# Who rounds and who subtracts the experts' weights: one engine fewer in the weight split of a mixture of experts

## The chip, the cores and the metric

One core of one Trainium2 chip. The metric is the device time of one execution in microseconds (us). Three runs of the kernel before give a median of 2515.39 us (2513.58 to 2515.87). All durations in this text are microseconds unless marked ns.

The engines are named as in the profile: PE is TensorE (PEld its weight loads), DVE is VectorE, ACT is ScalarE, POOL is GpSimd, SP is SyncE, which only issues DMAs here.

## What is computed

The reference runs two blocks over one sequence of 1024 tokens of width 1024. The first block is two layers of gating and sparse attention. The second is a windowed attention with a short convolution, and then a mixture of experts, which is where the change lies:

```
hierarchical_moe(h, ...):                      # 1024 tokens, 32 experts, top 2 of one group each
    expert, gates = router(h)                  # 2048 assignments of a token to an expert
    for e in range(32):
        xb  = h[tokens of expert e]            # gathered rows
        hid = silu(xb @ w_gate[e]) * (xb @ w_up[e])    # w_gate, w_up: 1024 x 256
        out[tokens of e] += gates * (hid @ w_down[e])  # w_down: 256 x 1024
```

Everything is in float32, and the weights are read once: 32 experts of three matrices of 1 MB.

## The kernel before, in words

**Products in parts.** A float32 product is made of three matmuls on rounded parts. Each operand is split into `hi`, its value rounded to the matmul's format, and `lo`, what is left of it. `mm3` (lines 99 to 102) then sums hi by hi, hi by lo and lo by hi; in the profile these are lines L100, L101 and L102. The split itself is the helper `split` (line 104): a rounding copy by POOL (L106), ACT (L108) or DVE, and then a subtraction, source minus hi, on L111 by DVE or POOL. All splits of the kernel share these lines, so the experts' splits are told apart by their tile, `ew`.

**The experts' stage** is the last fifth of the kernel. It runs from about 2050 to the end at 2515. For each expert:
- `load_e` (line 1506, its DMA on L1514) loads the three weight matrices, 1 MB each, through SP's queue into a ring of 11 places (`NRAW`). A load waits until its place is free, that is until both halves of the matrix loaded 11 loads earlier have been split, and until the third load before it has landed (`AHEAD = 3`).
- `gather` (L1604) fetches the expert's tokens, up to 96 rows, with an indirect DMA that POOL issues, three experts ahead.
- `prep` (line 1618) turns the tokens round with eight transposes (L1624), rounds them on ACT (L1626) and subtracts on DVE (L1627), into `xT`.
- `split_e` (line 1609) splits a weight matrix into a tile `ew`, of which there are three. It does so in two halves of 128 partitions by 1024 values. So there are six roundings and six subtractions per expert.
- `gate_up` (line 1630) makes the gate and up products, 48 matmuls of 256 columns into bank `sm`; ACT takes the tanh (L1638) and DVE finishes `th` (L1639, L1640).
- `hidden` (line 1645) transposes `th` (L1648), rounds (ACT, L1650) and subtracts (DVE, L1651) into `hdT`.
- `down` (line 1654) makes the down product, 12 matmuls of 512 columns into bank `big`; ACT scales the result into `yt` (L1663), and POOL issues the indirect DMA that adds its rows to the output (L1664, the scatter).

**Who splits what.** A counter `sc` goes round six places, one step per half:

```
HI_E = ("act", "act", "act", "pool", "act", "act")
        i = sc[0] % 6
        split(w_[:, 0, c], w_[:, 1, c], raw[:, c], HI_E[i], G if i in (1, 5) else V)
```

From the second expert on, the order of the calls puts each half of an expert in a fixed place. The second halves of gate and up are subtracted by POOL, and the second half of down is rounded by POOL; the other five roundings are ACT's and the other four subtractions DVE's.

**Order.** Each engine runs its instructions in a fixed order, one after the other. The program's order is expert by expert (`for e in range(NE)`, the loop behind `finish`): products of expert e, tokens and gate and up weights of e + 1, down product of e - 1, hidden part and down weights of e. The build (`schedule_with_timeline_sim=True`, line 1764) may shift instructions among each other by a simulated timeline of the engines, from which each engine's final order comes. After the loop stands a second one (`For_i`, over the blocks of experts with more than 96 tokens); with these inputs it is not entered: the profile shows 128 subtractions of DVE on `ew`, four for each of 32 experts.

Of the kernel before, what the change touches and what calls it, by code (L numbers as in the profile page):

```python
# [28 lines left out]
BIG = 1e30  # L29
SL = 96          # tokens of one expert's block  # L30
# [10 lines left out]
def tile_hybrid(ctx, tc, I, out):  # L41
# [7 lines left out]
    banks = {}  # L49
    psum2 = ctx.enter_context(tc.tile_pool(name="psum2", bufs=2, space=PSUM))  # L50

    def bank_plan(big, half, sm, tr, sc=0):
        """Banks of PSUM: big tiles of two, the others of one. Two small and two transposed ones stay in place."""
        if banks:
            banks["stack"].close()
        st = ExitStack()
        banks.update(stack=st, pool=st.enter_context(tc.tile_pool(name="psum", bufs=2, space=PSUM)),
                     big=big, half=half, sm=sm, tr=tr, sc=sc, turn={"sm": 0, "tr": 0})
# [54 lines left out]
    # weights are streamed two 128-row blocks at a time and split one step ahead of their use  # L113
# [11 lines left out]
    # the number of stages whose loads wait for an instruction, and which  # L125
# [33 lines left out]
    # background work, placed between the steps of a product. Generators in bgs yield about the time they take.  # L159
    # Streams hold the vector engine's long chains: they yield the time they take there and whether what comes next  # L160
    # starts on the tensor engine, which then must not come up before the chain is done. now is the tensor engine's
    # time so far, dve that up to which the vector engine has work.
# [97 lines left out]
    def dense_T1(KT, rhs, evac, bgt=1300.0):  # L260
        """One block of 128 channels: the halves take turns so that two banks last."""
        ps = [None, None]
        for k0 in range(0, KT, 4):
            hi, lo = wnext()
            hi, lo = (x.rearrange("p a b -> p (a b)").rearrange("p (k c) -> p k c", c=128) for x in (hi, lo))
            for h in range(2):
                c = slice(h * 512, (h + 1) * 512)
                if k0 == 0:
                    ps[h] = bank([128, 512], "half")
                for kk in range(4):  # L270
                    k = k0 + kk
                    mm3(ps[h], hi[:, kk], lo[:, kk], rhs(k, 0)[:, c], rhs(k, 1)[:, c], start=(k == 0),
                        stop=(k == KT - 1))
                if k0 + 4 == KT:
                    evac(h, ps[h])
                bg(bgt, 12 * 512 / 2.4)
# [14 lines left out]
    # every streamed weight, in the order of use  # L291
# [20 lines left out]
    # ------------------------------------------------------------------ block 1  # L312
# [9 lines left out]
    # rotary tables  # L322
# [29 lines left out]
    # modulation rows  # L352
# [13 lines left out]
    # first layer: scale and shift as columns, and h straight into its transposed halves. The products for 256 channels  # L366
    # of one of them are summed over row blocks by the vector engine, by the two slow ones or by the tensor engine.
# [77 lines left out]
    # later modulation rows: products summed over row blocks by the vector engine, over rows by one product with ones  # L445
# [63 lines left out]
    def rope(dst, src, t, H, eng):  # L509
        """Rotary embedding of H heads of 64 channels; t is one tile, or None for all tiles with one head each."""  # L510
        if t is None:
            cw, sw = cosT, sinT
        else:
            cw = cosT[:, t:t + 1, :].to_broadcast([128, H, 32])
            sw = sinT[:, t:t + 1, :].to_broadcast([128, H, 32])
        a, b = slice(0, 32), slice(32, 64)
        tb = tmp.tile([128, H, 64], FT, name="s2")
        eng.tensor_tensor(tb[:, :, a], src[:, :, b], sw, op=OP.mult)
        eng.tensor_tensor(tb[:, :, b], src[:, :, a], sw, op=OP.mult)
        for c in (a, b):  # L520
            eng.tensor_tensor(dst[:, :, c], src[:, :, c], cw, op=OP.mult)
        eng.tensor_tensor(dst[:, :, a], dst[:, :, a], tb[:, :, a], op=OP.subtract)
        eng.tensor_tensor(dst[:, :, b], dst[:, :, b], tb[:, :, b], op=OP.add)
# [35 lines left out]
    def layer(l, xin, hT=None):  # L559
# [6 lines left out]
        # keys, values, index keys and index weights  # L566
# [22 lines left out]
        # index queries  # L589
# [20 lines left out]
        def select(i):  # L610
            """Bias of query tile i: 0 at its 256 largest index scores, first ones on ties, else -BIG."""
# [30 lines left out]
            # upper halves of the scores as integers: they rise with the scores where these are non-negative and fall  # L642
            # where they are negative. With fewer than 256 non-negative scores the threshold is the (n - 255)-th from the
            # most negative one, and all non-negative ones count as larger.
# [22 lines left out]
            # lower halves of the scores that share the threshold's upper half; of these the K2-th largest, if among the  # L667
            # eight largest
# [29 lines left out]
        def choose(sc, gt, c, cand, z, eq=None, pre=None):  # L698
            """The 256 scores above the threshold with halves cand and c, first ones where equal."""
# [24 lines left out]
        def recheck(tiles):  # L724
            """Tiles with a threshold beyond the eight largest lower halves: these by bisection."""
# [38 lines left out]
        # spatial gating: v, u  # L764
# [7 lines left out]
        def sgu():  # L772
# [3 lines left out]
            # causal spatial weights, transposed  # L776
# [53 lines left out]
        # a unit's probabilities take one place of 1024, or two where there are more than 512 keys  # L830
# [88 lines left out]
        # queries  # L919
# [11 lines left out]
        # z_a: X = 2 * u * spatial gate * silu(z_a)  # L931
# [10 lines left out]
        # z_b, transposed  # L942
# [25 lines left out]
        # half the gate over alpha, and the weights of the output product  # L968
# [49 lines left out]
        def fin2(t, ya, yb, rt):  # L1018
            z = rt
            for h in range(2):  # L1020
                hs = slice(h * 512, (h + 1) * 512)
                py = bank([128, 512], "half")
                for i, (hi, lo) in enumerate((ya, yb)):
                    for k in range(4):
                        mm3(py, hi[:, k, :], lo[:, k, :], wo[i][:, 0, k, hs], wo[i][:, 1, k, hs],
                            start=(i, k) == (0, 0), stop=(i, k) == (1, 3))
                gy = tmp.tile([128, 512], FT, name="s2")
                V.tensor_tensor(gy, py, gate[h], op=OP.mult)
                (V if t == NT - 1 else G).tensor_tensor(z[:, hs], rt[:, hs], gy, op=OP.add)
            # the norm of alpha * x + gate * y, all over alpha  # L1030
            y = z
            norm(y, z, 1e-5 / ALPHA ** 2)
            e = V if t == NT - 1 else G
            y2 = y.rearrange("p (a b) -> p a b", a=2)
            e.tensor_tensor(y2, y2, ln[0], op=OP.mult)
            e.tensor_tensor(y2, y2, ln[1], op=OP.add)
            nc.sync.dma_start(xout[t * 128:(t + 1) * 128, :], y)
            if l == 0:
                h_tile(y, t, scale1, shift)
            else:  # L1040
                rms_tile(y, Xf[:, t, :], shift, Xf[:, t, :])
# [55 lines left out]
    # ------------------------------------------------------------------ block 2  # L1097
# [53 lines left out]
    def kv_prep():  # L1151
        """Values in two parts; keys with RMS norm and rotary embedding, doubled in X[:, :, 1, 256:512], transposed."""
# [135 lines left out]
    # short convolution on transposed channels  # L1288
# [31 lines left out]
    # gated merge, transposed: M = (1 + tanh) * projection, summed over both branches  # L1320
# [55 lines left out]
    # residual, second norm, router logits  # L1376
# [15 lines left out]
    # routing of one tile of tokens at a time: the two experts of each token, their gates, and the place of each  # L1392
    # assignment in its expert's list; assignment (k, token) is row 1024 k + token of Y
# [36 lines left out]
    def route(t, lg):  # L1430
# [45 lines left out]
        # gates  # L1476
# [7 lines left out]
        # slot + 1 in two exact parts, gate in three exact parts  # L1484
# [16 lines left out]
    # the experts' weights go round NRAW places, first where M was, then where its parts were  # L1501
# [70 lines left out]
    # ------------------------------------------------------------------ mixture of experts  # L1572
# [28 lines left out]
    sc = [0]  # L1601
# [5 lines left out]
    HI_E = ("act", "act", "act", "pool", "act", "act")  # L1607

    def split_e(raw):
        w_ = mo.tile([128, 2, 8 * 256], FR, name="ew", bufs=3)  # L1610
        for h in range(2):
            c = slice(h * 1024, (h + 1) * 1024)
            i = sc[0] % 6
            sc[0] += 1
            split(w_[:, 0, c], w_[:, 1, c], raw[:, c], HI_E[i], G if i in (1, 5) else V)
        return w_
# [83 lines left out]
    # experts with more than SL tokens: further blocks, in order; block i is block blk[i] + 1 of expert ex[i]  # L1700
# [78 lines left out]
```

## Time and profile before

| | |
|---|---|
| median of three runs | 2515.39 us |
| span of the profiled execution | 2515.2 us |
| experts' stage | about 2050 to 2515 |
| PE, DVE, POOL, ACT busy over the whole span | 87, 68, 52, 41% |
| DMA, mean over the span | 106 GB/s |

No separate device time is given for the profiled execution; its span, 2515.2, is taken for it. It stands 0.2 under the median, inside the range of the runs. The shares of busy time over the whole span mix many stages; for the change only those of the experts' stage matter, and they are quite different (DMA above all). A busy time counts an instruction from start to end, also while it is held up in the middle.

### The profile page before, as it was taken

How to read it: one execution, taken by the hardware profiler on the slowest of the kernel's cores; microseconds unless marked ns; L12 is line 12 of the kernel's file. 1: busy time of each engine (PE TensorE's matmuls, PEld its weight loads, DVE VectorE, ACT ScalarE, POOL GpSimd, SP SyncE). 2: the span in 40 equal slices, each digit the busy share in tenths (PEclk: the TensorE clock that was granted, in tenths of full speed). 3: DMA queues.
4: the chain of work that ended last, by engine and by line, in shares of the span. 5: the costliest groups of instructions: out<-in, count | busy, mean ns of one | idle time of the engine just before them, and what ended most of it. 6: DMA issues, size and time to landing. Idle time of an engine off the chain costs nothing. (4 is left out here: it accounts for less than half of the span.)

```text
span 2515.2 us, 36403 instructions
## 1 busy us (share of the span) xinstructions
PE 2194.3 (87%) x13235; PEld 1914.9 (76%) x13235; DVE 1705.0 (68%) x3475; ACT 1035.8 (41%) x1875; POOL 1301.4 (52%) x1102
## 2 busy tenths in 40 slices
PE   5997888699989898877998999999998977887885
PEld 5897886488779898766786988888886767776774
DVE  8689889877745879896786268730103357887885
ACT  4233333455532342435564346631212125554554
POOL 4755473456737525725553355432335137776775
PEclk9998999699999899988999999999999989998998
DMA  7522112211123111122211111121211649887893
GB/s 225 181 79 80 50 34 75 90 55 64 39 72 112 37 53 36 58 88 73 73 42 42 39 38 30 30 79 50 64 46 53 234 169 300 265 293 248 272 292 62
DMA packets 146509, 265.51 MB, mean 106 GB/s; under 512 B 23672, under 2 KB 100880, under 8 KB 134016
## 3 DMA queue, kind: packets, MB, share of 16 engines
q1 hardware_dynamic: 139136, 241.99, 29.6%
q0 software_dynamic: 7168, 20.98, 4.0%
q8 instruction: 105, 1.72, 0.3%
q14 instruction: 100, 0.82, 0.1%
HBM read 228.83 MB, written 38.29 MB: 106 GB/s over the span
## 5 line engine op out<-in xcount | busy, mean ns | idle before, releaser
L111 POOL TENSOR_TENSOR wlo<-wraw,whi 128x512 fp32r<-128x512 f32 (+1 forms) x188 | 254.3, 1353 | 490.8 <-ACT whi L108 472.8
L101 PE MATMUL big<-wlo,s 128*128 128x256 f32 (+1 forms) x1536 | 441.2, 289 | 12.8 <-POOL wlo L111 12.8
L100 PE MATMUL big<-whi,s 128*128 128x256 f32 (+1 forms) x1536 | 439.2, 289 | 11.4 <-ACT s L506 8.8
L102 PE MATMUL big<-whi,s 128*128 128x256 f32 (+1 forms) x1536 | 440.9, 289 | 0.0
L101 PEld LDWEIGHTS big<-wlo,s 128*128 128x128 f32 x1536 | 300.1, 196 | 17.8 <-POOL wlo L111 15.2
L100 PEld LDWEIGHTS big<-whi,s 128*128 128x128 f32 x1536 | 296.7, 195 | 18.9 <-ACT s L506 11.2
L102 PEld LDWEIGHTS big<-whi,s 128*128 128x128 f32 x1536 | 299.5, 195 | 2.8 <-issue 0.9
L108 ACT ACTIVATE whi<-wraw 128x512 fp32r<-128x512 f32 (+1 forms) x188 | 117.8, 628 | 419.6 <-PE big L102 143.4
L111 DVE TENSOR_TENSOR ew<-s,ew 128x1024 fp32r<-128x1024 f32 x91 | 209.1, 2321 | 16.9 <-POOL ew L106 9.6
L607 DVE TENSOR_SCALAR_CACHE_REDUCE junk<-up,cand 128x512 bf16<-128x512 int16 (+5 forms) x192 | 179.7, 936 | 1.4
L101 PE MATMUL sm<-ew,xT 128*96 128x256 f32 x512 | 153.8, 300 | 30.3 <-DVE ew L111 25.1
L637 DVE SCALAR_TENSOR_TENSOR s<-rel,widx,s 128x384 f32<-128x384 f32 (+3 forms) x140 | 132.4, 970 | 50.6 <-ACT rel L632 49.9
L102 PE MATMUL sm<-ew,xT 128*96 128x256 f32 x512 | 152.6, 298 | 4.2 <-DVE xT L1627 3.6
L100 PE MATMUL sm<-ew,xT 128*96 128x256 f32 x512 | 152.8, 299 | 0.5 <-ACT ew L108 0.5
L100 PE MATMUL half<-s,whi 128*128 128x512 f32 x320 | 133.1, 416 | 17.9 <-DVE s L950 11.0
L632 ACT ACTIVATE rel<-sm 128x384 f32<-128x384 f32 (+3 forms) x160 | 80.9, 524 | 159.6 <-PE sm L629 105.7
L111 POOL TENSOR_TENSOR ew<-s,ew 128x1024 fp32r<-128x1024 f32 x47 | 130.9, 2792 | 25.3 <-ACT ew L108 18.8
L101 PE MATMUL half<-s,whi 128*128 128x512 f32 x320 | 131.5, 411 | 0.0
L102 PE MATMUL half<-s,wlo 128*128 128x512 f32 x320 | 129.9, 410 | 0.3 <-POOL wlo L111 0.3
L108 ACT ACTIVATE ew<-s 128x1024 fp32r<-128x1024 f32 x116 | 115.5, 1049 | 22.5 <-PE sm L102 11.5
L101 PEld LDWEIGHTS sm<-ew,xT 128*96 128x96 f32 x512 | 89.9, 176 | 40.6 <-DVE ew L111 32.3
L862 POOL TENSOR_SCALAR Z<-Z,rc 128x128 f32<-128x128 f32 (+7 forms) x88 | 63.2, 730 | 109.1 <-DVE rc L860 74.6
(628 smaller groups left out, 6306.9 us busy)
## 6 DMA issues: line engine op xcount, KB each, us to landing
wraw<-in_w_in_dram SPq DMA_DIRECT2D x164, 256.0 KB, 2.9
adaw<-in_w_ada_dram SPq DMA_DIRECT2D x48, 512.0 KB, 4.1
s<-in_w_gate_e_dram SPq DMA_DIRECT2D x23, 1024.0 KB, 4.8
s<-in_w_up_e_dram SPq DMA_DIRECT2D x23, 1024.0 KB, 7.2
s<-in_w_down_e_dram SPq DMA_DIRECT2D x23, 1024.0 KB, 9.2
X<-in_w_gate_e_dram SPq DMA_DIRECT2D x9, 1024.0 KB, 6.7
X<-in_w_up_e_dram SPq DMA_DIRECT2D x9, 1024.0 KB, 6.8
X<-in_w_down_e_dram SPq DMA_DIRECT2D x9, 1024.0 KB, 8.6
```

Source lines behind the costliest of these rows:

```text
L100: T.matmul(o, lh, rh, start=start, stop=False, skip_group_check=True)
L101: T.matmul(o, lh, rl, start=False, stop=False, skip_group_check=True)
L102: T.matmul(o, ll, rh, start=False, stop=stop, skip_group_check=True)
L108: A.activation(hi, src, AF.Copy)
L111: return (sub or V).tensor_tensor(lo, src, hi.bitcast(FT), op=OP.subtract)
L607: V.tensor_scalar(junk[:, :src.shape[1]], src, thr, 0.0, op0=op, op1=OP.add, accum_out=cnt)
L632: A.activation(rel[:, :w_], ps[:, :w_], AF.Relu, scale=0.125)
L637: V.scalar_tensor_tensor(d, rel[:, :w_], widx[:, i, h:h + 1], d, op0=OP.mult, op1=OP.add)
L862: G.tensor_scalar(P[hh][:, :n], P[hh][:, :n], rc[:, hh:hh + 1], 1.0, op0=OP.mult, op1=OP.mult)
```

## The change

`split_e` no longer takes turns. Every half is rounded by ACT and subtracted by DVE. POOL keeps the two indirect DMAs per expert and nothing else in this stage. The counter and the table go away; all other hunks of the diff only remove comments.

```
-    sc = [0]
 
     def gather(tcol, b):
         ...
-
-    HI_E = ("act", "act", "act", "pool", "act", "act")
 
     def split_e(raw):
         w_ = mo.tile([128, 2, 8 * 256], FR, name="ew", bufs=3)
         for h in range(2):
             c = slice(h * 1024, (h + 1) * 1024)
-            i = sc[0] % 6
-            sc[0] += 1
-            split(w_[:, 0, c], w_[:, 1, c], raw[:, c], HI_E[i], G if i in (1, 5) else V)
+            split(w_[:, 0, c], w_[:, 1, c], raw[:, c], "act", V)
         return w_
```

## Rows read from the trace of the kernel before

**Rows 1.** The page: busy time of each engine, and the span in 40 equal slices of 63 us (each digit the busy share in tenths).

```profile
PE 2194.3 (87%) x13235; PEld 1914.9 (76%) x13235; DVE 1705.0 (68%) x3475; ACT 1035.8 (41%) x1875; POOL 1301.4 (52%) x1102
...
DVE  8689889877745879896786268730103357887885
...
POOL 4755473456737525725553355432335137776775
...
DMA  7522112211123111122211111121211649887893
```

**Rows 2.** Busy time by stretch: us of each engine with its instructions, the granted clock of TensorE, the share of the 16 DMA engines and what they moved. The stretches are the start, the middle and the end of the experts' stage, and two short ones in which the loads ran densely.

```profile
2050.00:2090.00 40.00, 23.89 (x168) 21.12 (x167) 25.55 (x69) 17.47 (x27) 25.32 (x19) 0.74 0.86 278
2090.00:2450.00 360.00, 289.52 (x1860) 251.27 (x1858) 293.33 (x251) 192.49 (x265) 255.96 (x131) 0.91 0.86 279
2450.00:2515.00 65.00, 38.55 (x251) 31.95 (x251) 39.01 (x32) 27.89 (x37) 39.04 (x18) 0.90 0.37 66
...
2090.00:2110.00 20.00, 13.97 (x90) 12.16 (x89) 18.81 (x15) 10.12 (x15) 16.86 (x9) 0.89 0.99 324
2200.00:2210.00 10.00, 6.79 (x46) 6.56 (x45) 7.38 (x7) 3.97 (x6) 4.57 (x4) 0.83 0.98 364
```

**Rows 3.** Groups of instructions in the stretch 2090 to 2450: line, engine, operation, out<-in, shape, count | busy us, mean ns of one | idle time of the engine before them, and what ended it.

```profile
L111 DVE TENSOR_TENSOR ew<-s,ew 128x1024 fp32r<-128x1024 f32 x78 | 180.6, 2340 | 12.9 <-POOL ew L106 7.1 <-ACT ew L108 5.6
...
L111 POOL TENSOR_TENSOR ew<-s,ew 128x1024 fp32r<-128x1024 f32 x39 | 107.3, 2758 | 23.7 <-ACT ew L108 17.6 <-PE tr L1624 4.8 <-POOL ew L106 0.9
L108 ACT ACTIVATE ew<-s 128x1024 fp32r<-128x1024 f32 x97 | 96.4, 1049 | 18.6 <-PE sm L102 10.7 <-issue 2.6 <-POOL ew L111 2.2
...
L111 DVE TENSOR_TENSOR ew<-X,ew 128x1024 fp32r<-128x1024 f32 x28 | 56.5, 2030 | 14.5 <-ACT ew L108 10.1 <-POOL ew L106 4.1
L1664 POOL DMA_INDIRECT out_dram<-yt,yi x25 | 48.9, 1954 | 5.9 <-issue 4.9 <-DVE xT L1627 0.6 <-DMA s<-in_w_down_e_dram 0.2
...
L111 POOL TENSOR_TENSOR ew<-X,ew 128x1024 fp32r<-128x1024 f32 x14 | 39.4, 2818 | 26.4 <-ACT ew L108 25.2 <-DMA s<-in_w_down_e_dram 1.1
...
L106 POOL TENSOR_SCALAR ew<-s 128x1024 fp32r<-128x1024 f32 x20 | 25.7, 1286 | 13.1 <-issue 12.6 <-PE big L102 0.5
...
L1638 ACT ACTIVATE th<-sm 96x256 f32<-96x256 f32 x26 | 9.9, 380 | 72.2 <-PE sm L102 72.2
L106 POOL TENSOR_SCALAR ew<-X 128x1024 fp32r<-128x1024 f32 x7 | 9.7, 1388 | 6.3 <-issue 6.3
```

**Rows 4.** The same stretch by the tile `ew`: duration in ns, least, median and most.

```profile
L111 DVE TENSOR_TENSOR ew<-s,ew x78: 1191/1225/6469, 2088.8 to 2448.6; 128x1024 fp32r<-128x1024 f32 x78
L111 POOL TENSOR_TENSOR ew<-s,ew x39: 2328/2614/3467, 2092.0 to 2449.2; 128x1024 fp32r<-128x1024 f32 x39
```

**Rows 5.** DVE and POOL side by side in two short stretches, in order of time: start, duration, engine, instruction, in brackets idle time before it. Of neighbours that are alike the durations are put together (x2).

```profile
2366.50 0.36 DVE L1651 TENSOR_TENSOR hdT<-tr,hdT 128x192 fp32r<-128x192 f32 x1 [3.33 <-ACT hdT L1650]
...
2382.51 1.23 DVE L111 TENSOR_TENSOR ew<-X,ew 128x1024 fp32r<-128x1024 f32 x1
2383.66 1.22 DVE L111 TENSOR_TENSOR ew<-s,ew 128x1024 fp32r<-128x1024 f32 x1
2384.79 3.42 DVE L111 TENSOR_TENSOR ew<-X,ew 128x1024 fp32r<-128x1024 f32 x1
2388.13 3.38 DVE L111 TENSOR_TENSOR ew<-s,ew 128x1024 fp32r<-128x1024 f32 x1
...
2363.66 1.45 POOL L1664 DMA_INDIRECT out_dram<-yt,yi  x1 [0.30 <-issue]
...
2381.43 1.05 POOL L106 TENSOR_SCALAR ew<-X 128x1024 fp32r<-128x1024 f32 x1 [4.32 <-issue]
2383.67 6.76 POOL L111 TENSOR_TENSOR ew<-s,ew 128x1024 fp32r<-128x1024 f32 x2 [1.19 <-ACT ew L108]
2390.60 2.25 POOL L1664 DMA_INDIRECT out_dram<-yt,yi  x1 [0.17 <-issue]
```

**Rows 6.** DMA in the stretch 2090 to 2450: the queues with packets, MB and share of the 16 engines, and a third of the loads with count, size and median us from issue to landing.

```profile
q1 hardware_dynamic: 11495, 83.76, 65.3%
q0 software_dynamic: 5614, 16.30, 20.5%
...
s<-in_w_down_e_dram SPq DMA_DIRECT2D x20, 1024.0 KB, 9.2
```

**Rows 7.** What SP's queue waited for in that stretch: us in total, times, longest.

```profile
SPq L1514 <- DVE ew L111: 244.5, 70, 8.5
SPq L1514 <- POOL ew L111: 63.3, 24, 4.7
```

**Rows 8.** The end: SP's last load, the tanhs of experts 28 and 31 on ACT and the last two scatters of POOL, in order of time.

```profile
2453.21 0.33 SPq L1514 DMA_DIRECT2D s<-in_w_up_e_dram  x1
...
2453.88 0.37 ACT L1638 ACTIVATE th<-sm 96x256 f32<-96x256 f32 x1
...
2489.87 0.38 ACT L1638 ACTIVATE th<-sm 96x256 f32<-96x256 f32 x1 [2.89 <-PE sm L102]
...
2496.67 1.42 POOL L1664 DMA_INDIRECT out_dram<-yt,yi  x1 [2.48 <-issue]
2502.82 1.41 POOL L1664 DMA_INDIRECT out_dram<-yt,yi  x1 [4.72 <-DMA out_dram<-yt,yi]
```

## The prediction, made before the changed kernel ran

> **What bounds the kernel now.** The page comes first, for where the change lies. Only the last fifth of its slices is concerned, and there DMA, at a fifth or less for most of the span, goes up to 8 and 9 tenths [rows 1]. Shares of the whole span say nothing on such a stage, so the view by stretches comes second. In the middle of the stage, 360 us, no engine is full: DVE is busy 293.3, PE 289.5, POOL 256.0, ACT 192.5 us, and the DMA engines have a share of 0.86 [rows 2]. That much was loaded in it as 83.76 MB, or 26.6 experts at 3.146 MB each [rows 6], so an expert takes 360/26.6 = 13.5 us.
>
> The third view, the groups of instructions, shows what is odd: one DVE subtraction on `ew` takes 2340 or 2030 ns in the mean [rows 3], but 1225 in the median and up to 6469 [rows 4]. A mean so far from the median is made of two kinds. The two timelines side by side show them. At 2382.51 and 2383.66 DVE subtracts in 1.23 and 1.22; the next two, of the same shape, take 3.42 and 3.38, and just then POOL makes two subtractions of its own in 6.76 [rows 5]. The surplus, 3.4 less 1.2, is about POOL's shortest time for one, 2328 ns [rows 4]. So the two engines' subtractions don't run beside each other: whichever comes second stands still, with its busy time counting on. POOL's rounding at 2381.43 took 1.05, others 1.5, with a mean of 1.29 to 1.39 [rows 3, 5]. DVE subtractions and POOL's together are one serial resource, and DVE's busy time is in large part standing.
>
> The fourth view says who pays. SP's queue waits 244.5 us for a DVE subtraction and 63.3 for one of POOL, over 94 waits [rows 7]: loads wait for a place that a late subtraction frees. And ACT's tanh waits 72.2 us for the products, which stand behind the remainders [rows 3]. DMA with 0.86 is the next limit, very near.
>
> **The change, part by part.** Per expert:
>
> *POOL's two subtractions go.* In the stretch these are 39 + 14 = 53, in 107.3 + 39.4 = 146.7 us, and 27 roundings in 35.4 us [rows 3]. What stays on POOL are the indirect DMAs, so nothing queues ahead of them any more.
>
> *DVE gets two more.* It goes from 106 subtractions in 237.1 us [rows 3] to 159. At the clean pitch, 1.14 from one start to the next (2382.51, 2383.66, 2384.79) [rows 5], these take 181. The rest of DVE's work is 293.3 - 237.1 = 56 [rows 2, 3]. So DVE falls from 293 to about 237 us although it does half as many subtractions again.
>
> *ACT gets one more rounding*, 27 x 1.05 = 28 us: from 192.5 to about 221 of 360 [rows 2, 3]. That lies beside other work as long as ACT isn't last; if it is, it costs 1.05 an expert, 34 us over 32 experts (the slower rival).
>
> *What is late next.* SP is freed from waiting for subtractions, and then the DMA engines set the pace. Their work is 0.86 x 360 = 310 us for the stretch [rows 2], 65.3% of the share from loads, 20.5% from gathers and scatters [rows 6]; the change leaves all of it. PE, 289.5 at a granted clock of 0.91, stays below.
>
> *How full can DMA run?* No row has a long stretch of it. In two short ones the share was 0.99 (20 us) and 0.98 (10 us) [rows 2]: the upper end, 310/0.98 = 316 us, a gain of 44. The lower end is the 0.86 of now, no gain. I take 0.95, nearer to the dense stretches because three loads may be under way and one takes 9.2 from issue to landing [rows 6], which covers the gaps: 310/0.95 = 326, **a gain of 34 us**. The stretch averages 279 GB/s, its densest ten microseconds 364 [rows 2]. The Trainium skill would make more of it: DMA: Bandwidth & Descriptors, section Bandwidth, gives 425 GB/s for a transfer of 16 MB; by it an expert's loads take 7.4 us, an estimate from that page, DMA would not be the limit, and the sum would be about 2425. No row here shows such a rate.
>
> *The end.* After the last load is issued at 2453.21 four experts are still to finish; tanhs of experts 28 and 31 are 36 us apart, 12.0 each [rows 8], with DMA at 0.37 [rows 2]. Here DVE and POOL set the pace, or PE. 289.5/26.6 x 0.91 = 9.9 us per expert is PE at full clock [rows 2]. Three steps from 12.0 to 10 give 6, and 2 from the last one; **8 us**. Its ends: nothing, if the last products keep their order with the scatters (each waits for the one before, [rows 8]), and 18 where compute has caught up with the loads and one expert less, another 9.9, is left over. From 2489.87, the last tanh, to the end, 25 us, stays.
>
> *The start*, 2050 to 2090, has a share of 0.86 and its first gathers ahead [rows 2]: 0.
>
> *Held issues.* The exclusion cuts the other way too. The scatter at 2363.66, with DVE idle, took 1.45; the one at 2390.60, beside a DVE subtraction, 2.25 [rows 5]. With half as many subtractions again on DVE more of the 64 indirect DMAs are held, 0.8 each: 51 us if every one lay on the path, nothing if none. Gathers are issued three experts ahead and little but the next scatter waits for a scatter, so I take 0. The Trainium skill has the rule behind it (GPSIMD Engine Reference, section Key points), and it speaks against more work on DVE: GpSimd shares its SBUF interfaces with VectorE and collides with instructions of two SBUF inputs. The trace agrees, in both directions; where the rule would give another sum, it is rival 5.
>
> The sum: 2515.2 (span, 0.2 under the median of 2515.39, so the two are taken as one) - 34 - 8 = **2473 us**.
>
> **The rivals.**
> 1. *Places are still freed late.* The ring of 11 places and the three `ew` tiles stay, and the down weights are split last as before. For it: SP waits for splits [rows 7], and a split needs a free `ew` tile, not DVE alone. Against: the standing time, 237 - 106 x 1.14 = 116 us, goes. DMA then gets to 0.90: 310/0.90 = 344, a gain of 16, with 5 at the end: 2494.
> 2. *Loads run faster than their share tells*, as they would if a packet's time grew with the packets that wait beside it. Then PE limits, at 10.5 us an expert (9.9 at full clock, and a little waiting): 26.6 x 3.0 = 80, and 10 at the end: 2425. For it: 364 GB/s moved at a share of 0.98 once. Against: only 324 at 0.99 [rows 2]. The Trainium skill's rate above would lead here.
> 3. *Slower: ACT sets the pace.* It runs in order, and all six roundings now stand in its queue ahead of the tanh, the token parts and `yt`. It already waits 72.2 us at the tanh [rows 3]. If its chain (rounding, product, tanh, rounding) is what lasts, 1.05 is added to each expert: 2515 + 34 = 2549. It decides once ACT's work and its waits for PE fill the 13.5 us; work alone is 221/26.6 = 8.3. Against: those waits are for products that themselves stand behind subtractions.
> 4. *No change.* The build makes each engine's order anew, by a simulated timeline that need not know of the exclusion. An order with more waits in it can eat the gain: 2515. The subtractions would be short and PE, ACT and SP would wait as long as before.
> 5. *Slower: held issues.* If every gather and scatter lay on the path and each were held 0.8, 51 us would stand against the 42: 2524. Against: the mean scatter already takes 1954 ns [rows 3], so most are held now. This is where the rule of the Trainium skill's GPSIMD Engine Reference would lead if taken to its end.
>
> **How the numbers follow.** The forecast, DMA sets the pace, has 0.57; rival 1 0.20; rival 2 0.08; rival 4 0.06; rival 3 0.06; rival 5 0.03. About 0.2%, 5 us, is what a measurement of this kernel can tell. Faster: 0.57 + 0.20 + 0.08 = 0.85; same 0.06; slower 0.06 + 0.03 = 0.09. The forecast's own range, with 0.90 to 0.98 of DMA share and 0 to 18 at the end, is 2453 to 2499. For 8 in 10 it has to take in rival 1 and reach towards rivals 2 and 4: 2442 to 2512. That leaves out rival 2 with 0.08, most of rival 4 and the two slower ones.
>
> **What would show it.** In the profile of after every subtraction on `ew` by DVE should take about 1.2, none over 2.5, and there should be 192 of them. DVE's busy time in the stage should fall, ACT's rise by about 30 us. The stage's DMA share should be 0.93 or more, and SP's waits should turn from subtractions to landed loads. If the subtractions are short and the share stays under 0.9, it is rival 1 or 4; if ACT is busy or waiting throughout and the tanhs are further apart than 13.5, rival 3. The forecast is wrong from the start if subtractions stay long with POOL idle: then it wasn't POOL that held them.

## The result, and the profile after

The changed kernel takes 2437.28 us (median of 4 runs, 2434.67 to 2440.49) against 2514.48 of the kernel before on the same chip: a ratio of 0.9699, interval 0.9688 to 0.9711. It is faster by 77 us, where 42 were forecast; 2437.3 lies under the lower end of the range, 2442. The profiled execution took 2434.67, its span is 2432.7. Disturbed runs are left out of every time below, and where the profiled execution itself was one (the paced dummies, 2756 us at a granted clock of 0.74), its rows are read only for what stood and what waited for what.

The subtractions first, by the tile `ew` (least, median, most in ns), from 2090 to the last load of this profile. These answer to [rows 4]:

```profile
L111 DVE TENSOR_TENSOR ew<-s,ew x124: 1211/1219/1229, 2088.9 to 2383.1; 128x1024 fp32r<-128x1024 f32 x124
...
L111 DVE TENSOR_TENSOR ew<-X,ew x46: 1212/1220/1228, 2109.3 to 2385.3; 128x1024 fp32r<-128x1024 f32 x46
```

The two kinds are gone. 170 subtractions lie between 1211 and 1229 ns, and over the whole stage there are 192. The groups by line tell the same as busy time, against [rows 3]:

```profile
L111 DVE TENSOR_TENSOR ew<-s,ew 128x1024 fp32r<-128x1024 f32 x124 | 146.3, 1221 | 29.9 <-ACT ew L108 28.7 <-issue 0.2
...
L111 DVE TENSOR_TENSOR ew<-X,ew 128x1024 fp32r<-128x1024 f32 x46 | 54.2, 1220 | 11.1 <-ACT ew L108 10.9
L1659 POOL DMA_INDIRECT out_dram<-yt,yi x26 | 51.2, 1968 | 116.1 <-DMA out_dram<-yt,yi 68.2 <-ACT ew L108 17.7 <-ACT hdT L1645 14.9
...
L1633 ACT ACTIVATE th<-sm 96x256 f32<-96x256 f32 x29 | 11.0, 379 | 20.5 <-PE sm L102 20.5
```

DVE makes 170 subtractions in 146 + 54 = 200 us, where 106 took 237. ACT's tanh waits 20.5 us for products, not 72.2. The view by stretches, against [rows 2] (busy us of PE, PEld, DVE, ACT, POOL, then granted clock, DMA share and GB/s):

```profile
2050.00:2090.00 40.00, 21.13 (x137) 18.89 (x136) 25.05 (x68) 15.74 (x23) 11.97 (x13) 0.66 0.90 295
2090.00:2387.00 297.00, 278.26 (x1972) 246.85 (x1972) 256.21 (x323) 231.56 (x309) 77.17 (x52) 0.99 1.01 337
2387.00:2433.00 46.00, 24.50 (x158) 20.18 (x158) 18.61 (x25) 19.24 (x25) 8.91 (x6) 0.83 0.43 83
```

The middle stretch is shorter by 66 us, from 2090 to the last load at 2387.06 and not 2453.21 [rows 8]. PE is busy for 278 of 297 us, at a granted clock of 0.99, so next to the upper of its two levels (2.4 GHz) throughout; before it was 0.91, with 290 of 360 busy [rows 2]. And the DMA engines have a share of 1.01 and move 337 GB/s, where 279 went before. The queues, and what SP waited for, against [rows 6, 7]:

```profile
q1 hardware_dynamic: 11358, 82.70, 75.1%
q0 software_dynamic: 5824, 17.03, 25.3%
```

```profile
SPq L1514 <- DMA s<-in_w_down_e_dram: 56.9, 17, 5.0
SPq L1514 <- DMA s<-in_w_gate_e_dram: 53.2, 16, 4.6
SPq L1514 <- DMA s<-in_w_up_e_dram: 49.0, 18, 4.1
...
SPq L1514 <- DVE ew L111: 13.2, 10, 2.7
```

SP waits for loads that are under way, hardly for subtractions (13.2 us, before 244.5). The end, against [rows 8]:

```profile
2387.06 0.33 SPq L1514 DMA_DIRECT2D s<-in_w_up_e_dram  x1
...
2376.28 0.38 ACT L1633 ACTIVATE th<-sm 96x256 f32<-96x256 f32 x1 [0.86 <-PE sm L102]
...
2406.10 0.37 ACT L1633 ACTIVATE th<-sm 96x256 f32<-96x256 f32 x1
...
2414.27 1.41 POOL L1659 DMA_INDIRECT out_dram<-yt,yi  x1 [4.92 <-issue]
2420.42 1.41 POOL L1659 DMA_INDIRECT out_dram<-yt,yi  x1 [4.74 <-DMA out_dram<-yt,yi]
```

From the last load to the end of the span there were 62 us, now 46. The tanh of expert 28 came 0.7 us after that load; now it comes 10.8 ahead of it. The four last tanhs are 29.8 us apart, before 36.

### The profile page after: what moved, and what is told of

Its sections match the earlier page's. It is cut to its first block, busy times and chain, and to the rows that moved or that the text cites. A ratio compares the mean times of both kernels' runs of the same rounds, so it can differ in the third digit from the quotient of the medians.

```text
span 2432.7 us, 36229 instructions
## 1 busy us (share of the span) xinstructions
PE 2165.2 (89%) x13235; PEld 1895.6 (78%) x13235; DVE 1649.2 (68%) x3539; ACT 1065.5 (44%) x1907; POOL 1081.0 (44%) x1006
## 5 line engine op out<-in xcount | busy, mean ns | idle before, releaser
L111 DVE TENSOR_TENSOR ew<-s,ew 128x1024 fp32r<-128x1024 f32 x138 | 162.8, 1221 | 35.0 <-ACT ew L108 33.7
L108 ACT ACTIVATE ew<-s 128x1024 fp32r<-128x1024 f32 x138 | 137.8, 1049 | 25.3 <-PE sm L102 16.3
L100 PE MATMUL sm<-ew,xT 128*96 128x256 f32 x512 | 146.6, 286 | 2.0 <-ACT xT L1621 2.0
L102 PE MATMUL sm<-ew,xT 128*96 128x256 f32 x512 | 147.3, 288 | 0.6 <-DVE xT L1622 0.6
L101 PE MATMUL sm<-ew,xT 128*96 128x256 f32 x512 | 145.3, 284 | 0.8 <-DVE ew L111 0.7
L1659 POOL DMA_INDIRECT out_dram<-yt,yi x32 | 60.1, 1878 | 149.9 <-DMA out_dram<-yt,yi 86.5
L629 PE MATMUL sm<-kist,qT 128*128 128x384 f32 (+3 forms) x320 | 91.2, 376 | 14.4 <-ACT rel L632 13.0
```

The lines of the kernel that those rows point to most:

```text
L100: T.matmul(o, lh, rh, start=start, stop=False, skip_group_check=True)
L101: T.matmul(o, lh, rl, start=False, stop=False, skip_group_check=True)
L102: T.matmul(o, ll, rh, start=False, stop=stop, skip_group_check=True)
L108: A.activation(hi, src, AF.Copy)
L111: return (sub or V).tensor_tensor(lo, src, hi.bitcast(FT), op=OP.subtract)
L629: T.matmul(ps[:, :w_], qT[g][:, j, :], kist[a][:, p * w_:(p + 1) * w_], start=a == 0, stop=a == 1)
```

## The experiments

Ratios are against the kernel before on the same chip, with their 95% interval. Two theories stood against each other. **Exclusion**: while POOL works on SBUF, a DVE subtraction stands. **Late remainders**: POOL is only slow, and TensorE waits for what it makes.

**The operations alone.** A kernel that leaves out the whole reference and runs the disputed operations alone and side by side on tiles of their own:

```
for fs in ([(dsub, 12)], [(gsub, 6)], [(dsub_1, 12), (gsub2, 6)], [(dsub_2, 12), (ground, 12)],
           [(dsub_3, 12), (gfill, 12)], [(dpsum, 24), (gsub3, 6)], [(around, 12), (dcopy, 16), (gsub4, 6)]):
    section()          # waits for all that came before
    ...
loads_1(); loads_2(); loads_3(); loads_5(); loads_3s()
```

> A kernel of its own that computes nothing of the reference: stretches of the disputed operations alone and side by side on tiles that do not depend on each other, then only loads of expert weights, with 1, 2, 3 and 5 under way, and 3 with scatters beside them. Exclusion: 12 subtractions of DVE with 6 of POOL beside them take 12 x 1.14 + 6 x 2.33 = 28 us, not the 14 of the longer alone, and DVE's are of two kinds, 1.2 and 3.4; beside 12 roundings of POOL 26 us; beside fills of POOL 14; DVE's subtractions from PSUM and copies, and ACT's roundings, are not held. POOL only slow: 14 us in each. Loads: if the share of 0.95 that the forecast took was only too low, three under way give about 340 GB/s at a share of 1.0 or more, and five give no more; one gives about 220.

The lines by source, least/median/most in ns and first and last start in us. First DVE alone and POOL alone, then both; then DVE with POOL's roundings, DVE with POOL's fills, and DVE's subtractions from PSUM and its copies, each beside six subtractions of POOL:

```profile
L74 DVE TENSOR_TENSOR od<-src,hi x12: 1218/1218/1224, 17.5 to 30.0; 128x1024 fp32r<-128x1024 f32 x12
L83 POOL TENSOR_TENSOR og<-src,hi x6: 2335/2336/2340, 42.6 to 54.0; 128x1024 fp32r<-128x1024 f32 x6
L104 DVE TENSOR_TENSOR od<-src,hi x12: 1211/2290/3361, 67.7 to 93.0; 128x1024 fp32r<-128x1024 f32 x12
L86 POOL TENSOR_TENSOR og<-src,hi x6: 3314/3317/3379, 67.7 to 84.2; 128x1024 fp32r<-128x1024 f32 x6
L107 DVE TENSOR_TENSOR od<-src,hi x12: 1212/2052/2103, 105.6 to 127.4; 128x1024 fp32r<-128x1024 f32 x12
L110 DVE TENSOR_TENSOR od<-src,hi x12: 1218/1220/1226, 139.9 to 152.4; 128x1024 fp32r<-128x1024 f32 x12
L77 DVE TENSOR_TENSOR od<-ps,hi x24: 548/548/558, 165.0 to 175.7; 128x384 fp32r<-128x384 f32 x24
L80 DVE COPY of<-src x16: 685/694/2734, 189.5 to 212.6; 128x1024 f32<-128x1024 f32 x16
```

Alone a subtraction takes DVE 1218 ns and POOL 2336. Together both have the same 3.3 to 3.4 us while the other works, and 12 and 6 of them end after 26.6 us: the two engines take strict turns, one instruction each. POOL's roundings cost DVE a turn too (2052). Fills, which read nothing, cost nothing (1220). Subtractions whose source is in PSUM are not held (548). DVE's copies of one SBUF input are, from 0.69 to 2.73, which the expectation had wrong. ACT's roundings beside them are not (1042). Exclusion is shown, for work of POOL that reads SBUF. The rows agree with the Trainium skill (GPSIMD Engine Reference, section Key points: contention with VectorE instructions in a 2-port mode or with two SBUF inputs), and they show it as turns of whole instructions, not as a slower pace of both.

The same kernel then only loads. The view by stretches (busy us of DVE, ACT and POOL, then granted clock, DMA share, GB/s): one load under way with scatters beside it, one alone, then two, three, five and three:

```profile
250.00:270.00 20.00, 0.00 (x0) 0.00 (x0) 5.13 (x4) 1.00 0.98 261
310.00:350.00 40.00, 0.75 (x5) 0.00 (x0) 0.00 (x0) 1.00 0.60 210
390.00:410.00 20.00, 0.00 (x0) 0.00 (x0) 0.00 (x0) 1.00 0.99 406
470.00:490.00 20.00, 0.00 (x0) 0.00 (x0) 0.00 (x0) 1.00 1.02 423
570.00:590.00 20.00, 0.00 (x0) 0.00 (x0) 0.00 (x0) 1.00 1.01 421
670.00:690.00 20.00, 0.00 (x0) 0.00 (x0) 0.00 (x0) 1.00 1.01 422
```

Three under way give 423 GB/s, not the 340 expected, and five no more. A full set of engines reads as 1.01 or 1.02 in this view. The scatters ran beside the first loads, not the last as meant: there a share of 0.98 is only 261 GB/s. So how much a full share moves hangs on what is moved. (The expectation had about 220 for one load under way; it is 210.)

**One part of the change alone.** Two kernels, each with half of the change:

```
+            split(w_[:, 0, c], w_[:, 1, c], raw[:, c], "pool" if i == 3 else "act", V)              # subtractions moved
+            split(w_[:, 0, c], w_[:, 1, c], raw[:, c], "act", G if i in (1, 5) else V)              # rounding moved
```

> The kernel after, but POOL keeps its one rounding per expert (second half of the down weights); only the two subtractions are moved to DVE. Theory 1, exclusion (a DVE subtraction stands while POOL works elementwise on SBUF): one stand of about 1.05 us per expert is left, DVE's chain is 6 x 1.14 + 2.3 + 1.05 = 10.2 us per expert, level with the 10.2 at which the tanhs of the changed kernel follow each other: 2437 to 2450. Theory 2, POOL is only slow (its remainders come late, nothing stands): 2437 to 2445 too. Theory 3, the gain comes from the rounding that left POOL or from a luckier order: 2480 or more.

> The kernel before, but the rounding is moved from POOL to ACT; POOL keeps its two subtractions per expert. Theory 1, exclusion: two stands of 2.33 us per expert are left, the serial chain of DVE and POOL falls only from 12.4 to about 11.5 us: 2485 to 2505, and the subtractions of DVE are still of two kinds, 1.2 and 3.4. Theory 2, POOL only slow: 2500 to 2515. Theory 3, the rounding was what mattered: about 2440.

With the subtractions moved alone: 2437.9, ratio 0.9682 (0.964 to 0.9723), the whole gain. With the rounding moved alone: 2476.5, 0.9843 (0.98 to 0.9886), half of it, more than either theory gave it. DMA then gets to 0.94 and POOL is still busy for 218 of 297 us, as the view by stretches shows (columns as in the changed kernel's, and so below):

```profile
2090.00:2387.00 297.00, 254.19 (x1729) 222.12 (x1729) 243.75 (x232) 201.88 (x271) 218.18 (x99) 0.95 0.94 312
```

The two halves don't add. With one turn of POOL an expert left, the rounding's 1.05 us, nothing of the gain is missing; with two left, half of it is. So the rounding is not what mattered by itself: left alone it costs nothing, and beside the subtractions half of the gain. Why the halves add up so unevenly is not shown.

**POOL as busy, but reading nothing.** The kernel before, with fills in place of POOL's subtractions; the remainders of those halves are left out:

```
             if i in (1, 5):
+                A.activation(w_[:, 0, c], raw[:, c], AF.Copy)
+                for _ in range(2):
+                    G.memset(w_[:, 1, c].bitcast(FT), 0.0)
```

> The kernel before, but POOL's two subtractions per expert are each replaced by two fills of the same tile (the remainders of those halves are left out); the table, POOL's rounding and POOL's time, about 2 us each, stay. Exclusion by POOL's reading: most of the gain comes, 2437 to 2465. POOL's time or its late remainders: 2490 to 2515.

2437.6, ratio 0.9706 (0.9645 to 0.9767), as fast as the changed kernel. POOL was busy nearly as long as with the rounding moved, but PE for 278 us and DMA at 1.01, as in the changed kernel:

```profile
2090.00:2387.00 297.00, 278.03 (x1978) 249.89 (x1977) 195.16 (x263) 205.99 (x282) 213.44 (x194) 0.98 1.01 336
```

So POOL's time as such was not the cost. But a fill waits for no rounding, so no remainder is late, and it reads no weights, so no place is held until POOL is done. The next run brings the reading back without the lateness.

**Standing without lateness.** The kernel after, with POOL's old subtractions made once more for nobody:

```
             split(w_[:, 0, c], w_[:, 1, c], raw[:, c], "act", V)
+            if i in (1, 5):
+                for j in range(3):
+                    q = slice(h * 1024 + 341 * j, h * 1024 + 341 * j + 342)
+                    G.tensor_tensor(dmy, raw[:, q], w_[:, 0, q].bitcast(FT), op=OP.subtract)
```

> The kernel after, and POOL also makes the two subtractions per expert of the kernel before, from the same weights and the same rounded halves, each in three parts of 128x342, into a scratch tile that nobody reads. PE no longer gets any remainder from POOL, so nothing is late; only the standing is brought back (and the places and tiles are held until POOL is done, as before). Exclusion: DVE's chain is 6 x 1.14 + 2.3 + 2 x 2.4 = 13.9 us per expert, 2500 to 2550. The gain came from POOL's remainders being late for PE: 2437 to 2450.

2516.4, ratio 0.9996 (0.998 to 1.0013). The gain is gone, though no product waits for a subtraction of POOL's. So late remainders are not needed for the loss. The number is the one that exclusion gave, but the path is not the one named with it, DVE's chain. DVE's subtractions on `ew` did stand (medians of 1.38 and 1.68 us), but the loads waited for POOL, as the waits of SP's queue from 2330 to 2690 show:

```profile
SPq L1514 <- POOL dmy L1619: 257.7, 54, 8.4
SPq L1514 <- DVE ew L111: 38.6, 17, 4.7
```

In the kernel before it was the other way round, 244.5 for DVE and 63.3 for POOL [rows 7]. The dummies were long because they too stood in turn: 1.4 us in the median, 0.91 the shortest. So this run does not part DVE's standing from places and `ew` tiles that are held until POOL is done; the fills can't do it either, since they hold no place. That DVE's standing was the larger part in the kernel before is read from its waits [rows 7]; no run has the one without the other.

**Two coarser dummies** came first, and told less:

```
+                for _ in range(3): G.tensor_tensor(dmy, one, one, op=OP.subtract)      # 128x352, twice an expert
+                for _ in range(6): G.memset(dmy, 0.0)                                  # the other kernel
```

> The kernel after, and POOL makes, beside the experts' second halves of gate and up, subtractions that nobody reads: three of 128x352 with two SBUF inputs for each half, six per expert, about as long together as the two that it made before. No result waits for them. Theory 1, exclusion: DVE's six subtractions stand behind them, the chain is 6 x 1.14 + 2.3 + about 5 = 14 us per expert: 2530 to 2580, slower than the kernel before, and DVE's subtractions are of several kinds again. Theory 2, POOL only slow: the time stays at 2437, and the subtractions at 1.22.

> The kernel after, and POOL fills a scratch tile that nobody reads, twelve memsets of 128x352 per expert, which write SBUF and read nothing. Exclusion by POOL's reading: the time stays at 2437 and DVE's subtractions at 1.22. Exclusion by any elementwise work of POOL on SBUF: subtractions stand, 2480 to 2560. POOL only slow: 2437.

The subtractions gave 2540.5, 1.0097 (1.0062 to 1.0131), as exclusion said. But the reason is not the one given. DVE's subtractions on `ew` stood little (medians of 1421 and 1290 ns, at most 1890); it was POOL's that stood, in turn with DVE's, as the tile of the dummies and the view by stretches show:

```profile
L1620 POOL TENSOR_TENSOR dmy<-one x192: 765/795/4372, 2058.4 to 2381.2; 128x352 f32<-128x352 f32 x192
```

```profile
2090.00:2380.00 290.00, 212.97 (x1318) 185.58 (x1317) 201.97 (x219) 153.35 (x208) 272.78 (x213) 0.86 0.75 241
```

They take from 0.77 up to 4.37 us, POOL was busy 273 of 290, and its scatters came late: ACT's `yt` waited 108 us for them. The fills gave 2458.2, 0.9768 (0.9726 to 0.981), against both theories: they wait for nothing that others make, ran early and stood ahead of the indirect DMAs in POOL's queue. DVE's subtractions kept their 1.22, and ACT's `yt` waited 46.7 us for scatters from 2090 to 2330, in the changed kernel 5.6 from 2090 to 2387. What is issued there pays for what stands in front of it.

**How many loads under way.** `AHEAD = 3` in the kernel after, changed to 2 and to 5:

> The kernel after with two loads under way in place of three. Loads set the pace of the changed kernel and are dense only because three overlap: the share falls under 0.95, 2445 to 2480. PE sets the pace: 2437.

> The kernel after with five loads under way in place of three. The DMA engines are full at a share of 1.01: 2434 to 2440, no change. If the wait for the third load before still costs: 2420 to 2432, a better version.

Two: 2453.1, 0.9744 (0.9695 to 0.9793), with a share of 0.96 and 307 GB/s from 2094 to 2380: loads do pace it. Five: 2450.8, 0.9746 (0.9703 to 0.9789), slower than three, which nothing had forecast. The share is 0.99 and as much is moved, 334 GB/s; tanhs are 10.2 apart nearly throughout until 2319 and then up to 15.8. Why more loads in the queues cost is open.

**Less to load, less to add.** In the kernel after the down weights' loads are left out (the down products use the gate weights' bytes), or the scatters, or only the scatters' empty rows:

```
-            wds[e] = split_e(raws.pop(e)[2])                          # two loads an expert
+            wds[e] = split_e(raws.pop(e)[0])
-        return G.indirect_dma_start(out=out, ..., compute_op=OP.add)  # no scatters
-    G.iota(spare, pattern=[[0, 1]], base=S + 1, ...)                  # empty rows skipped
+    G.iota(spare, pattern=[[0, 1]], base=2 * S + 1, ...)
```

> The kernel after without the loads of the down weights: the down products use the gate weights' bytes, so a third of the loads is left out, and all splits and products stay. If loads hold back the changed kernel only at its end (tanhs 10.2 us apart up to the twentieth expert, then 10.9 in the mean): every expert takes 10.2, 2422 to 2430. If they pace it throughout: 2400 or less. If they do not hold it at all: 2437.

> The kernel after without the scatters (the experts' results are not added to the output). If the DMA engines' whole work paces it: the scatters' share goes, 10.2 us per expert to the end and a shorter end, 2410 to 2425. If the loads alone count and the scatters run beside them: only the last scatter's landing goes, about 2427.

> The kernel after, and the empty places of an expert's block (96 places, 64 tokens in the mean) get a row index beyond the output, so that the scatters leave those rows out; before they went to spare rows. 1024 of 3072 rows of 4 KB, a third of the scatters' bytes, go. If the DMA engines' work paces the last ten experts of the changed kernel: about 18 us of DMA work go, nearly as good as leaving a third of the loads out: 2426 to 2434, a better version. If only loads count or an index out of bounds costs as much as a row: 2437.

Two loads: 2424.6, 0.9632 (0.9599 to 0.9664). No scatters: 2416.0, 0.9605 (0.9563 to 0.9646). The first lies where DMA was to hold the kernel back only late, the second where its whole work was to count. The view by stretches of the one, then of the other:

```profile
2094.00:2380.00 286.00, 270.94 (x1942) 241.19 (x1940) 252.68 (x317) 228.77 (x305) 65.78 (x53) 1.00 0.83 252
```

```profile
2094.00:2380.00 286.00, 272.64 (x1943) 242.76 (x1941) 253.89 (x318) 228.58 (x305) 24.38 (x25) 0.99 0.87 313
```

The share falls to 0.83 and 0.87, and PE is as busy as before. The tanhs of the changed kernel, beside those of the one without scatters, in the same part of the stage (the timeline of ACT):

```profile
2257.07 0.38 ACT L1633 ACTIVATE th<-sm 96x256 f32<-96x256 f32 x1 [0.82 <-PE sm L102]
...
2267.26 0.38 ACT L1633 ACTIVATE th<-sm 96x256 f32<-96x256 f32 x1 [0.81 <-PE sm L102]
...
2277.81 0.38 ACT L1633 ACTIVATE th<-sm 96x256 f32<-96x256 f32 x1 [0.82 <-PE sm L102]
...
2287.99 0.38 ACT L1633 ACTIVATE th<-sm 96x256 f32<-96x256 f32 x1 [0.82 <-PE sm L102]
...
2298.94 0.38 ACT L1633 ACTIVATE th<-sm 96x256 f32<-96x256 f32 x1 [0.82 <-PE sm L102]
...
2310.32 0.38 ACT L1633 ACTIVATE th<-sm 96x256 f32<-96x256 f32 x1 [0.82 <-PE sm L102]
...
2322.79 0.36 ACT L1633 ACTIVATE th<-sm 96x256 f32<-96x256 f32 x1
```

```profile
2294.51 0.38 ACT L1633 ACTIVATE th<-sm 96x256 f32<-96x256 f32 x1 [0.81 <-PE sm L102]
...
2304.69 0.38 ACT L1633 ACTIVATE th<-sm 96x256 f32<-96x256 f32 x1 [0.82 <-PE sm L102]
...
2314.88 0.38 ACT L1633 ACTIVATE th<-sm 96x256 f32<-96x256 f32 x1 [0.82 <-PE sm L102]
...
2325.06 0.38 ACT L1633 ACTIVATE th<-sm 96x256 f32<-96x256 f32 x1 [0.82 <-PE sm L102]
```

With less on the queues they stay 10.2 apart until the last; in the changed kernel they do up to 2267, and the next are 10.6, 10.2, 11.0, 11.4 and 12.5 apart. So 10.2 us is PE's pace in its order (from 2180 to 2270 it was busy for 86.7 of 90 us), and DMA comes in late. From the first tanh to the last it is 324.0 us, and 317.1 and 317.5 without the one or the other: 7 us is what DMA still costs there. Most of the rest of the scatters' 21 is at the end, where the span goes on 26.6 us after the last tanh, and 12.7 without them. Skipping the empty rows brought nothing: 2436.3, 0.9674 (0.9649 to 0.9698). The loads moved no faster (82.21 MB in the stretch from 2090 to 2387, 82.70 with the empty rows), though the scatters' queue fell from 17.03 to 13.60 MB. Why a third of the scatters' bytes is worth nothing here is not shown.

**The same elsewhere.** The kernel after, with the remainders of the second block's streamed weights (`wlo`) subtracted by DVE too:

> The kernel after, and in the second block ahead of the experts the remainders of the streamed weights (128x512, tile wlo) are subtracted by DVE too, not by POOL. The exclusion carries over: DVE stands less there, but PE is the bound of those stretches at 8 to 9 tenths and waits little for remainders: 2425 to 2437. If DVE becomes late for its other work: up to 2460.

2440.1, 0.9694 (0.9661 to 0.9726): no gain on the changed kernel. No version that beats the changed kernel was found.

## Why the prediction was wrong

**Right: what bounds the kernel.** The reading of two kinds of subtraction as POOL and DVE in turns is shown by the operations alone. That it was the cost follows from three findings: with POOL's subtractions moved, the whole gain is there; with POOL as busy but reading nothing, too; and loads, which had waited 244.5 us for DVE's subtractions [rows 7], waited 13.2. How the cost was shared between DVE's standing and places held by POOL itself stays open. DVE's busy time fell, ACT's rose by 29 us over the stage, the subtractions are 192 of 1.2, SP's waits turned to loads. Each sign named ahead came.

**Wrong: how full DMA can run.** The failed step is the 34 us. The work of the stretch, 310 us, was divided by a share of 0.95, with 0.98 as the upper end. The share was 1.01. Full reads as 1.01 to 1.02 in this view, as the loads alone show. With 1.01 the step gives 310/1.01 = 307, 19 us more. The two short stretches at 0.98 and 0.99 [rows 2] were not the ceiling but nearly so.

**Wrong: that this work was fixed.** 83.76 MB of loads took 65.3% of 360 us [rows 6], 2.81 us of all engines per MB; after it is 75.1% of 297 for 82.70 MB, 2.70. The work of the stretch was not the 310 us of before but 1.01 x 297 = 300, which is another 10; about 3 of these are one load of 1 MB less in the stretch, the rest is what each MB took. It goes by how many loads are under way. Alone, a MB takes 2.86 with one (0.60 of the time at 210 GB/s), 2.44 with two and 2.40 with three or five. In the changed kernel it takes 2.81 with two, 2.70 with three and 2.68 with five. So a share of 0.86 was not an amount of work that stays when the loads stand closer. Why a MB takes less then is not shown. 34, 19 and 10 make 63; the 3 us up to 66 are those from 2450, where the stretch of the prediction ended, to the last load at 2453.

The Trainium skill's rate, 425 GB/s (DMA: Bandwidth & Descriptors, section Bandwidth), is borne out where loads run alone, 421 to 423; the mix with gathers and scatters moves 337 at a full share. The prediction was right not to count on that rate.

**Left out: the stock.** The forecast had one pace, DMA's. There were two. Loads went at 297/26.3 = 11.3 us an expert in the mean (82.70 MB), tanhs at 10.2, and both at once: the 11 places hold 3.7 experts' weights, and PE, faster by one us an expert, lives on what has landed ahead. The timelines of SP and ACT count it. At each tanh from the second to the tenth expert, ten loads were issued beyond those of that expert; at the nineteenth, at 2267, seven; from the twenty-fifth, at 2332, five or six, of which three may be under way. Without the scatters there are ten until no load is left to issue. That the tanhs slow down after 2267 because of it is an inference, borne out by the two kernels with less on the queues, in which they don't slow down. The share was 1.02 from 2100 to 2180 already, where PE set the pace: a full share alone does not say that DMA is what is waited for.

Rival 2 had PE's pace nearly right, 10.5, and 2437 lies nearer to its 2425 than to 2473. Its reason came in part: the loads ran faster than their share told. But a MB takes less with more beside it, and the rival had it the other way round.

**Right in kind, low in size: the end.** 8 were forecast, with 0 to 18 as ends; 16 came. The step of 6 from 12.0 to 10 an expert was 6.2. The rest is what the upper end said, that compute catches up with the loads: expert 28 stands 11.5 us earlier against the last load, and 1.3 are lost again after the last tanh.

Together: 34 + 8 forecast; 66 + 16 in the spans, 82.5, of which the medians show 77. The profiled execution was the quickest of four, 2.6 under the median. And its span is 2.0 under its time; for the kernel before the prediction had taken the two for one, so its profiled execution will have stood some 2 us above the median (an estimate).

**The rivals.** The slower ones had no part. ACT was busy 231.6 of 297 us; DVE's subtractions waited 39.6 us for its roundings, but PE's products only 2. The order did not spoil the gain: the tanhs came at 10.2 us for a dozen experts on end. Held issues went against what the prediction said of them. It expected more of them, with more subtractions on DVE. The scatters over the whole stage (least, median, most in ns), before and after:

```profile
L1664 POOL DMA_INDIRECT out_dram<-yt,yi x32: 1406/2232/2432, 2095.6 to 2502.8; - x32
```

```profile
L1659 POOL DMA_INDIRECT out_dram<-yt,yi x32: 1407/1630/5262, 2095.2 to 2420.4; - x32
```

The mean in the middle stretch stayed, 1954 [rows 3] and 1968, because three of them took 3.1 to 5.3 us; the median fell from 2.23 to 1.63. So they were held less, not more, and the 0 that the forecast took for it was right by another way.

## What to carry to other kernels

An instruction's mean that stands far from its median points to two kinds of instruction; put the timelines of the engines that share something with it side by side. Work handed to GpSimd to relieve VectorE costs VectorE its own time, if both read SBUF: here two subtractions and a rounding of POOL per expert cost 77 us of 2514, and taking away the subtractions was enough. When one limit goes, don't cap the next one at a share read from short stretches, and don't take its share for a fixed amount of work: ask what a full one reads like, what stock lies in front of it, and which pace comes after.

## What the runs showed of the hardware that was not expected

- POOL stands as DVE does: in strict turns its subtraction took 3.32 us beside DVE's where 2.34 stood alone, and its rounding up to 2.01 where the shortest was 1.05. DVE's copies of one SBUF input took part too.
- The DMA view's share went to 1.02. Loads alone moved 423 GB/s at it, the experts' mix 337, loads with scatters one by one 261 at 0.98.
- The engine time of a MB of loads fell with the number under way: 2.86, 2.44 and 2.40 us with one, two and three.
- Five loads under way in place of three made the kernel slower by 13 us at nearly the same rate of transfer, 334 and 337 GB/s.
